# Filter chunks that write into their own inputs, in 512-column steps and with other gaps between them, and a Hyena result that is split in two halves

## The chip, the cores and the metric

The kernel runs on one core of one Trainium2 chip. The metric is the device time of one execution in microseconds (us), the median of the runs.

## What is computed

Two layers of a bidirectional encoder trunk on 256 positions of width 1024, all in float32. Each layer is a mixer and a SwiGLU feed-forward part, with an RMSNorm ahead of and behind each. Cut to what the change touches:

```python
def implicit_filters(L, w1, b1, fr1, w2, b2, fr2, w3):
    z, t = filter_features(L)
    h = jnp.sin(fr1.astype(jnp.float32) * (z @ w1.astype(jnp.float32) + b1.astype(jnp.float32)))
    h = jnp.sin(fr2.astype(jnp.float32) * (h @ w2.astype(jnp.float32) + b2.astype(jnp.float32)))
    h = (h @ w3.astype(jnp.float32)).reshape(L, 2 * HYENA_ORDER, HYENA_WIDTH).transpose(1, 2, 0)
...
    return h * decay[None]

def bidir_fft_conv(z, h_fwd, h_bwd, bias):
...
    kf = jnp.fft.rfft(k, axis=-1).T
    zf32 = z.astype(jnp.float32)
    zf = jnp.fft.rfft(zf32, n=2 * L, axis=1)
    y = jnp.fft.irfft(zf * kf[None], n=2 * L, axis=1)[:, :L]
    return (y + zf32 * bias.astype(jnp.float32)).astype(z.dtype)

def hybrid_mixer(u, pos, w_in, conv_w, conv_b, fw1, fb1, ff1, fw2, fb2, ff2, fw3, hy_bias,
                 w_o_attn, w_o_hyena, w_gate, b_gate, w_out):
...
    proj = u @ w_in
...
        o, l = dilated_window_attention(q[:, :, g], k[:, :, g], v[:, :, g], dil, window // (2 * dil))
...
    filt = implicit_filters(S, fw1, fb1, ff1, fw2, fb2, ff2, fw3)
    z = hx1 * bidir_fft_conv(hv, filt[0], filt[1], hy_bias[0])
    z = hx2 * bidir_fft_conv(z, filt[2], filt[3], hy_bias[1])
    y_hy = z @ w_o_hyena
...
    merged = gates[:, :, 0] * y_att.astype(jnp.float32) + gates[:, :, 1] * y_hy.astype(jnp.float32)
    return merged.astype(u.dtype) @ w_out
```

## The kernel before

**The main stream.** TensorE (PE) multiplies the activations by the weights in 128-row pieces, in the order in which the program is written. Every float32 product is three matmuls: high part by high part, high by low, low by high. A piece of weights comes by a DMA that SyncE (SP) issues (`raw`, L140, a ring of four buffers), ScalarE (ACT) makes its high part (`whi`, `hi_of`, L86), and VectorE (DVE) the low part (`wlo`, `lo_of`, L89); while `shared` holds, every fifth low part is made by GpSimd (POOL). The pieces of a projection into columns are 128x1024 (`wa`), those of q, k and v 128x768 (`wq`), worked off as 12 matmuls of 384 columns.

**The side jobs.** The filters, the FFT convolutions and the attention are generators. `tick()` (L98), which the main stream calls once for each piece, moves at most two of them on to their next `yield`. So the number of yields is the number of pieces that TensorE works off between two steps of a job. TensorE stays in program order; the instructions of DVE, ACT, POOL and SP are put in order by a scheduler when the kernel is built, and each engine then works off its list strictly in that order.

**A filter chunk** (`filter_chunk`, L280; for each layer four column groups `cc` and two filters `v`). SP loads `w3` (tile `w`, L282) and, into a single buffer, the bias row `bb` (L289). POOL makes the sum and the difference of the two halves of `w3` (`sd`, L294, L298), ACT and another engine split them (`sh`, `sl`, L303: DVE in layer 0, POOL in layer 1). The step "gst" (L309, L310) multiplies by the hidden features, DVE multiplies by the decay (`dd`, L313) and splits (`dh`, `dl`). The step "Z" (L326) is the transform by `fd`; `ev` (L330, L332) takes `bb` up, and four additions write the spectrum `K` (L335 to L339). Chunks with `l == 1 and cc == 2` (`late`) have four pieces ahead of gst, all others two; two pieces stand between gst and Z. The chunks of layer 0 run beside layer 0's first projections, those of layer 1 with `cc` 0 and 1 beside the feed-forward part of layer 0 and the rest beside the start of layer 1's mixer.

**A convolution** (`conv`, L539): POOL folds (`eo`, L543, L544), TensorE transposes (L549) and transforms (L559), DVE multiplies by `K` (L563 to L565), POOL adds (L566, L567, both 128x256), TensorE transforms back (L576, tile `inv`), POOL multiplies by the next factor (`X`, L584).

**An attention slot** (`attend`, L610): scores, softmax on DVE and ACT (`S`, L635 to L640), three pieces later the transposes of `S` (L648), then the product with v. The rotary embedding (`rt`, `qk`, L603 to L608) is POOL's. Ahead of slot 3 the whole Hyena result `X2` is split by `z_split` (L741): `zh` on ACT, `zl` on DVE, two halves of 128x1024.

Of the kernel before, what the change touches and what calls it, by code (L numbers as in the profile page):

```python
# [21 lines left out]
F32R = mybir.dt.float32r  # L22
BF16 = mybir.dt.bfloat16
AF = mybir.ActivationFunctionType
OP = mybir.AluOpType
# [19 lines left out]
def trunk(tc, nc, a, out):  # L45
# [4 lines left out]
    with es:  # L50
# [229 lines left out]
        def filter_chunk(l, v, cc, K, fd, shared):  # L280
# [22 lines left out]
            lo_of(sl, sd, sh, nc.gpsimd if l else None)  # L303
            for _ in range(4 if late else 2):
                yield
            Dh, Dl = [], []
            for e in range(2):
                h = acc()
                mm(h, gst[l][:, e, :], sh, True, False)  # L309
                mm(h, gst[l][:, e, :], sl, False, True)  # L310
                d = t512("dd")
                for q in range(2):
                    vtt(d[:, q * 256:(q + 1) * 256], h[:, q * 256:(q + 1) * 256], dec[:, e, :], op=OP.mult)  # L313
                dh, dl = r512("dh"), r512("dl")
                hi_of(dh, d)
                lo_of(dl, d, dh)
                Dh.append(dh)
                Dl.append(dl)
            yield
            yield  # L320
            hh, cq = cc // 2, cc % 2
            for s in range(2):
                z = acc()
                for e in range(2):
                    b = (2 * s + e) * P
                    mm3(z[:, e * 256:(e + 1) * 256], fd[:, b:b + P], fd[:, 512 + b:512 + b + P],  # L326
                        Dh[e][:, s * 256:(s + 1) * 256], Dl[e][:, s * 256:(s + 1) * 256], True, True)
                ev = f256("ev")
                if s == 0:
                    vtt(ev, z[:, 0:256], bb, op=OP.add)  # L330
                else:
                    nc.scalar.activation(ev, z[:, 0:256], AF.Copy)  # L332
                k0 = K[v][0][hh][:, cq * 512 + s * 256: cq * 512 + s * 256 + 256]
                k1 = K[v][1][hh][:, cq * 512 + s * 256: cq * 512 + s * 256 + 256]
                vtt(k0, z[:, 256:512], ev, op=OP.add)  # L335
                if s == 0:
                    vtt(k1, ev, z[:, 256:512], op=OP.subtract)
                else:
                    vtt(k1, z[:, 256:512], ev, op=OP.subtract)  # L339
            yield  # L340
# [198 lines left out]
        def conv(v, cc, z, xg, K):  # L539
# [16 lines left out]
            for j in range(2):  # L556
# [7 lines left out]
                vtt(t2[:, 0:256], zz[:, 0:256], Kt[:, 256:512], op=OP.mult)  # L564
                vtt(t2[:, 256:512], zz[:, 256:512], Kt[:, 0:256], op=OP.mult)  # L565
                ptt(t1[:, 0:256], t1[:, 0:256], t1[:, 256:512], op=OP.subtract)  # L566
                ptt(t1[:, 256:512], t2[:, 0:256], t2[:, 256:512], op=OP.add)  # L567
# [17 lines left out]
            yield  # L585
            yield
# [23 lines left out]
        def attend(s, qk, vt, OT):  # L610
# [30 lines left out]
            yield  # L641
            yield
            yield
# [30 lines left out]
        def mixer(l, U, o, K):  # L674
# [29 lines left out]
            convs = [4]  # L704
            X1 = [bigt(name="X1") for h in range(2)]
            X2 = [bigt(name="X2") for h in range(2)]
            for cc in range(4):
# [9 lines left out]
                def both(cc=cc, hvc=hvc, x1c=x1c, x2c=x2c):  # L717
                    yield from conv(0, cc, hvc, x1c, K)
                    yield from conv(1, cc, x1c, x2c, K)
                    convs[0] -= 1  # L720

# [17 lines left out]
            ZH, ZL = [], []  # L739

            def z_split():  # L741
                for h in range(2):
                    zh, zl = bigt(F32R, name="zh"), bigt(F32R, name="zl")
                    hi_of(zh, X2[h])
                    lo_of(zl, X2[h], zh)
                    ZH.append(zh)
                    ZL.append(zl)


            for s in (2, 3):  # L750
                att = slot(s, [bigt(name="qk") for i in range(2)], z_split if s == 3 else None)
# [242 lines left out]
```

## Time and profile before

| | |
|---|---|
| time, median of 3 runs (lowest to highest) | 1100.67 us (1100.32 to 1102.95) |
| the profiled execution | 1101.53 us |
| its span, first to last instruction | 1099.8 us |
| TensorE busy | 1077.7 us, 98% of the span |
| VectorE, ScalarE, GpSimd busy | 712.9, 554.0 and 394.1 us |
| mean granted TensorE clock | 0.998 of full speed |

The profiled execution lies 0.86 us above the median. TensorE is busy nearly all the time, so a change shows in the time only through the gaps in TensorE's work. A row of a timeline gives the start and the length of an instruction, or of a run of like ones (`x4`), and in brackets how long its engine was idle before it and what ended that.

### The profile page before, as it was taken

The page shows a single profiled execution, that of the slowest core. Times are in us where ns is not written, and L with a number is a line of the kernel's source. Part 1 is how long each engine was busy: PE and PEld are TensorE (multiplying, and loading weights), DVE is VectorE, ACT ScalarE, POOL GpSimd, SP SyncE. Part 2 cuts the span into 40 slices and gives each one's busy share as a digit, 9 for nine tenths or more (in the row PEclk, how much of TensorE's full clock was granted, in tenths as well). Part 3 has the DMA queues.
Part 4 walks back from the last instruction along what each step waited for, and adds up shares of the span by engine and source line. Part 5 has one row for each costly group of instructions (what it writes and reads, how often), then busy time and mean ns, then how long its engine had stood idle before and what let it go on. Part 6 is the DMA issues. An engine that isn't in the chain of part 4 may idle for free.

```text
span 1099.8 us, 18234 instructions
## 1 busy us (share of the span) xinstructions
PE 1077.7 (98%) x6984; PEld 1005.5 (91%) x6984; DVE 712.9 (65%) x1131; ACT 554.0 (50%) x828; POOL 394.1 (36%) x480
## 2 busy tenths in 40 slices
PE   8989999999999999999999999999999999999997
PEld 7989998899888899999889999998999889999986
DVE  5799986656646756665475877876445676554554
ACT  6555564443644645454465564444355455544442
POOL 2543123578713134211116714466645220111110
PEclk9999999999999999999999999999999999999999
DMA  8566544444446555656655544444455466555662
GB/s 295 177 207 196 163 140 141 151 132 128 145 163 199 185 183 185 194 179 222 198 171 172 179 148 141 133 158 150 129 158 187 164 219 191 156 189 177 206 192 77
DMA packets 60881, 189.21 MB, mean 172 GB/s; under 512 B 6903, under 2 KB 9337, under 8 KB 60794
## 3 DMA queue, kind: packets, MB, share of 16 engines
q1 hardware_dynamic: 60794, 188.04, 53.3%
q8 instruction: 55, 0.90, 0.3%
q14 instruction: 32, 0.26, 0.1%
HBM read 186.97 MB, written 1.05 MB: 171 GB/s over the span
## 4 chain that ended last, share of the span: by engine, by line
PE 88%; DVE 6%; DMA 2%; ACT 2%; issue 1%; POOL 1%; SPq 0%; DVEq 0%; POOLq 0%; ACTq 0%
PE acc L78 84%; DVE wlo L89 2%; PE acc L618 1%; DVE dl L89 1%; DMA mask<-in_mask_dram 1%; DVE dd L313 1%; ACT jk L350 1%; DMA raw<-in_wq_dram 1%; ACT whi L86 1%; PE acc L549 1%; PE acc L395 1%; PE acc L648 1%; DVE arg L239 1%; DMA w<-in_w_dram 0%; DVE X L371 0%
## 5 line engine op out<-in xcount | busy, mean ns | idle before, releaser
L86 ACT ACTIVATE whi<-raw 128x1024 fp32r<-128x1024 f32 (+1 forms) x352 | 346.3, 991 | 384.7 <-PE acc L78 292.0
L89 DVE TENSOR_TENSOR wlo<-raw,whi 128x1024 fp32r<-128x1024 f32 (+1 forms) x294 | 345.3, 1182 | 227.0 <-ACT whi L86 224.1
L78 PE MATMUL acc<-UH,whi 128*128 128x256 f32 x992 | 282.4, 285 | 0.0
L78 PE MATMUL acc<-UH,wlo 128*128 128x256 f32 x992 | 280.6, 283 | 0.0
L78 PE MATMUL acc<-UL,whi 128*128 128x256 f32 x992 | 280.6, 283 | 0.0
L89 POOL TENSOR_TENSOR wlo<-raw,whi 128x1024 fp32r<-128x1024 f32 (+1 forms) x58 | 132.9, 2292 | 405.2 <-ACT whi L86 405.1
L78 PE MATMUL acc<-whi,UH 128*128 128x384 f32 (+1 forms) x576 | 204.6, 355 | 0.0
L78 PE MATMUL acc<-wlo,UH 128*128 128x384 f32 (+1 forms) x576 | 202.0, 351 | 2.2 <-DVE wlo L89 1.4
L78 PE MATMUL acc<-whi,UL 128*128 128x384 f32 (+1 forms) x576 | 200.6, 348 | 0.0
L78 PEld LDWEIGHTS acc<-UL,whi 128*128 128x128 f32 x992 | 190.2, 192 | 0.4
L78 PEld LDWEIGHTS acc<-UH,whi 128*128 128x128 f32 x992 | 190.1, 192 | 0.4
L78 PEld LDWEIGHTS acc<-UH,wlo 128*128 128x128 f32 x992 | 190.1, 192 | 0.0
L78 PEld LDWEIGHTS acc<-wlo,UH 128*128 128x128 f32 x576 | 109.0, 189 | 9.8 <-DVE wlo L89 4.1
L78 PEld LDWEIGHTS acc<-whi,UH 128*128 128x128 f32 x576 | 109.1, 189 | 5.6 <-issue 0.7
L78 PEld LDWEIGHTS acc<-whi,UL 128*128 128x128 f32 x576 | 108.8, 189 | 5.4 <-DVE UL L89 0.2
L78 PE MATMUL acc<-whi,hs 128*128 128x512 f32 x352 | 109.0, 389 | 0.0
L78 PEld LDWEIGHTS acc<-whi,hs 128*128 128x128 f32 x352 | 66.1, 188 | 13.7
L78 PE MATMUL acc<-wlo,hs 128*128 128x512 f32 x176 | 68.5, 389 | 0.0
L828 DVE TENSOR_TENSOR HF<-acc,silu 128x256 f32<-128x256 f32 x38 | 16.1, 424 | 48.4 <-PE acc L78 48.4
L357 POOL TENSOR_SCALAR nv<-ss 128x1 f32<-128x1 f32 x16 | 7.1, 442 | 105.2 <-ACT jk L350 105.2
L78 PEld LDWEIGHTS acc<-wlo,hs 128*128 128x128 f32 x176 | 33.1, 188 | 6.7
L567 POOL TENSOR_TENSOR t<-t 128x256 f32<-128x256 f32 x32 | 36.5, 1142 | 4.3 <-DVE t L565 2.3
(168 smaller groups left out, 1570.1 us busy)
## 6 DMA issues: line engine op xcount, KB each, us to landing
raw<-in_wa_dram SPq DMA_DIRECT2D x240, 512.0 KB, 4.0
raw<-in_wq_dram SPq DMA_DIRECT2D x96, 384.0 KB, 3.5
raw<-in_wg_dram SPq DMA_DIRECT2D x16, 384.0 KB, 3.7
w<-in_w_dram SPq DMA_DIRECT2D x16, 256.0 KB, 4.2
gain<-in_gains_dram SPq DMA_DIRECT2D x7, 512.0 KB, 6.8
dec<-in_dec_dram SPq DMA_DIRECT2D x8, 256.0 KB, 3.1
bb<-in_hyb_dram SPq DMA_DIRECT2D x16, 128.0 KB, 3.3
gb<-in_bg_dram SPq DMA_DIRECT2D x8, 256.0 KB, 3.7
```

The lines of the kernel that those rows point to most:

```text
L78: nc.tensor.matmul(o, lT, r, start=start, stop=stop)
L86: return nc.scalar.activation(o, i, AF.Copy)
L89: (eng or nc.vector).tensor_tensor(o, i, h, op=OP.subtract)
L239: stt(arg, k, -c, arg, op0=OP.mult, op1=OP.add)
L313: vtt(d[:, q * 256:(q + 1) * 256], h[:, q * 256:(q + 1) * 256], dec[:, e, :], op=OP.mult)
L350: nc.scalar.activation(jk, half, AF.Square, scale=D ** -0.5, accum_out=ss[:, h:h + 1])
L395: nc.tensor.transpose(t[:, q * P:(q + 1) * P], u[:, h * 512 + q * P: h * 512 + (q + 1) * P], ident)
L549: nc.tensor.transpose(t[:, q * P:(q + 1) * P], eo[:, q // 2, q % 2, :], ident)
L567: ptt(t1[:, 256:512], t2[:, 0:256], t2[:, 256:512], op=OP.add)
L618: nc.tensor.transpose(t[:, q * P:(q + 1) * P], qk[i][:, j * 384 + g * P: j * 384 + (g + 1) * P], ident)
L648: nc.tensor.transpose(t[:, q * P:(q + 1) * P], S[:, i * 512 + q * P:i * 512 + (q + 1) * P], ident)
L828: vtt(ct(HF, f), ob, sl, op=OP.mult)
```

## The change

In `filter_chunk` the decayed product `dd` has no tile of its own: the first goes into `sd`, the second into `w`, and each is one 512-column instruction in place of two of 256. `ev` is one 512-column tile, and `K` is written by two 512-column instructions in place of four of 256. `sl` is made by POOL in both layers. The pieces ahead of gst and between gst and Z become 4 and 4 for `late` chunks, 3 and 3 in layer 0, and stay 2 and 2 for the other chunks of layer 1; the yield at the end goes in layer 0. In `conv` two 256-column products become one of 512 columns, and the two yields at the end stay for `v == 0` alone. Attention slot 2 gets a fourth piece between the softmax and the transposes. `z_split` takes one half: the first when two of the four convolution jobs are done, the second ahead of slot 3.

```diff
@@ filter_chunk
-            lo_of(sl, sd, sh, nc.gpsimd if l else None)
-            for _ in range(4 if late else 2):
+            lo_of(sl, sd, sh, nc.gpsimd)
+            for _ in range(4 if late else 2 if l else 3):
                 yield
             Dh, Dl = [], []
             for e in range(2):
                 h = acc()
                 mm(h, gst[l][:, e, :], sh, True, False)
                 mm(h, gst[l][:, e, :], sl, False, True)
-                d = t512("dd")
-                for q in range(2):
-                    vtt(d[:, q * 256:(q + 1) * 256], h[:, q * 256:(q + 1) * 256], dec[:, e, :], op=OP.mult)
+                d = (sd, w)[e]
+                vtt(d[:, :].rearrange("p (q c) -> p q c", q=2), h[:, :].rearrange("p (q c) -> p q c", q=2),
+                    dec[:, e:e + 1, :].to_broadcast([P, 2, 256]), op=OP.mult)
                 dh, dl = r512("dh"), r512("dl")
...
-            yield
-            yield
...
+            for _ in range(4 if late else 2 if l else 3):
+                yield
+
+            Z = []
+            for e in range(2):
                 z = acc()
...
+                for s in range(2):
+                    b, c = (2 * s + e) * P, slice(s * 256, (s + 1) * 256)
+                    mm3(z[:, c], fd[:, b:b + P], fd[:, 512 + b:512 + b + P], Dh[e][:, c], Dl[e][:, c], True, True)
+                if e == 0:
+                    ev = t512("ev")
+                    nc.scalar.activation(ev[:, 256:512], z[:, 256:512], AF.Copy)
+                    vtt(ev[:, 0:256], z[:, 0:256], bb, op=OP.add)
+                Z.append(z)
+
+            c = slice((cc % 2) * 512, (cc % 2) * 512 + 512)
+            vtt(K[v][0][cc // 2][:, c], Z[1], ev, op=OP.add)
+            vtt(K[v][1][cc // 2][:, c], ev, Z[1], op=OP.subtract)
+            if l:
+                yield
@@ conv
-                vtt(t2[:, 0:256], zz[:, 0:256], Kt[:, 256:512], op=OP.mult)
-                vtt(t2[:, 256:512], zz[:, 256:512], Kt[:, 0:256], op=OP.mult)
...
+                zv, kv, tv = (x.rearrange("p (s c) -> p s c", s=2) for x in (zz[:, :], Kt, t2[:, :]))
+                vtt(tv, zv, kv[:, ::-1, :], op=OP.mult)
...
-            yield
-            yield
+            if v == 0:
+                yield
+                yield
@@ attend
-            yield
-            yield
-            yield
+            for _ in range(4 if s == 2 else 3):
+                yield
@@ mixer
+            def z_split(h):
+                zh, zl = bigt(F32R, name="zh"), bigt(F32R, name="zl")
+                hi_of(zh, X2[h])
+                lo_of(zl, X2[h], zh)
...
                     convs[0] -= 1
+                    if convs[0] == 2:
+                        z_split(0)
...
-                att = slot(s, [bigt(name="qk") for i in range(2)], z_split if s == 3 else None)
+                att = slot(s, [bigt(name="qk") for i in range(2)], (lambda: z_split(1)) if s == 3 else None)
```

The scheduler also moves instructions whose code is unchanged. The first place is SP's list at the start of layer 1's mixer, where the last filter chunks are loaded: `w3` is the weights of a chunk, `bb` its bias row, `raw` a piece of the main stream. Before:

```order
L282 DMA w3_6852<-in_w3_dram 128x512 [waits Pool_49]
L140 DMA raw_6894<-in_wq_dram 128x768 [waits DMAHW1_49,DVE_49]
L282 DMA w3_6865<-in_w3_dram 128x512 [waits Pool_49]
L727 DMA gb_8307<-in_bg_dram 128x512 [waits DVE_49]
L140 DMA raw_6952<-in_wq_dram 128x768 [waits DMAHW2_49,DVE_49]
L289 DMA bb_6588<-in_hyb_dram 128x256 [waits DMAHW3_49,DVE_49]
L140 DMA raw_6988<-in_wq_dram 128x768 [waits DMAHW4_49,Pool_49]
L289 DMA bb_6856<-in_hyb_dram 128x256 [waits DMAHW5_49,DMAHW3_49,DVE_49]
```

And of the change:

```order
L140 DMA raw_6902<-in_wa_dram 128x1024 [waits DMAHW6_49,DVE_49]
L289 DMA bb_6488<-in_hyb_dram 128x256 [waits DMAHW4_49,DVE_49]
L282 DMA w3_6774<-in_w3_dram 128x512
L289 DMA bb_6778<-in_hyb_dram 128x256 [waits DMAHW4_49,DVE_49]
L282 DMA w3_6787<-in_w3_dram 128x512 [waits DMAHW7_49]
L140 DMA raw_6958<-in_wa_dram 128x1024 [waits DMAHW0_49,DVE_49]
```

The two `w3` of layer 1's `cc == 3` stood ahead of both `bb`; now each stands behind one, and a `bb` waits on DVE until the `ev` before it has read the single buffer.

The second place is POOL's list a little later, where the same two chunks are made ready for gst; `rt` is the rotary embedding of an attention slot. Before:

```order
L294 TENSOR_TENSOR sd_6869<-w3_6865 128x256
L298 TENSOR_TENSOR sd_6869<-w3_6865 128x256
L89 TENSOR_TENSOR wlo_6837<-raw_6834,whi_6836 128x768
L89 TENSOR_TENSOR sl_6862<-sd_6858,sh_6861 128x512
L89 TENSOR_TENSOR sl_6873<-sd_6869,sh_6872 128x512
L603 TENSOR_TENSOR rt_6817<-qk_6655,rope_87 128x48
```

And of the change:

```order
L298 TENSOR_TENSOR sd_6791<-w3_6787 128x256
L89 TENSOR_TENSOR sl_6784<-sd_6780,sh_6783 128x512
L605 TENSOR_TENSOR rt_6817<-qk_6555,rope_87 128x48
L606 TENSOR_TENSOR rt_6817<-qk_6555,rope_87 128x48
L607 TENSOR_TENSOR rt_6817<-qk_6555,rope_87 128x48
L608 TENSOR_TENSOR rt_6817<-qk_6555,rope_87 128x48
L605 TENSOR_TENSOR rt_6825<-qk_6556,rope_87 128x48
L606 TENSOR_TENSOR rt_6825<-qk_6556,rope_87 128x48
L607 TENSOR_TENSOR rt_6825<-qk_6556,rope_87 128x48
L608 TENSOR_TENSOR rt_6825<-qk_6556,rope_87 128x48
L89 TENSOR_TENSOR wlo_6887<-raw_6884,whi_6886 128x768
L89 TENSOR_TENSOR sl_6795<-sd_6791,sh_6794 128x512
```

Both `sl` stood ahead of the rotary embedding; now the second one stands behind eight of its instructions and a `wlo`.

The third place is POOL's list in layer 0, at the first convolutions (`v == 0`) of `cc` 2 and 3; L566 and L567 before are L564 and L566 or L568 after. Before:

```order
L566 TENSOR_TENSOR t1_2918<-t1_2918 128x256
L567 TENSOR_TENSOR t1_2918<-t2_2919 128x256
L566 TENSOR_TENSOR t1_2932<-t1_2932 128x256
L567 TENSOR_TENSOR t1_2932<-t2_2933 128x256
L566 TENSOR_TENSOR t1_2964<-t1_2964 128x256
```

And of the change:

```order
L564 TENSOR_TENSOR t1_2907<-t1_2907 128x256
L605 TENSOR_TENSOR rt_2932<-qk_2652,rope_87 128x48
L606 TENSOR_TENSOR rt_2932<-qk_2652,rope_87 128x48
L607 TENSOR_TENSOR rt_2932<-qk_2652,rope_87 128x48
L608 TENSOR_TENSOR rt_2932<-qk_2652,rope_87 128x48
L568 TENSOR_TENSOR t1_2894<-t2_2895 128x256
L605 TENSOR_TENSOR rt_2940<-qk_2653,rope_87 128x48
L606 TENSOR_TENSOR rt_2940<-qk_2653,rope_87 128x48
L607 TENSOR_TENSOR rt_2940<-qk_2653,rope_87 128x48
L608 TENSOR_TENSOR rt_2940<-qk_2653,rope_87 128x48
L566 TENSOR_TENSOR t1_2907<-t2_2908 128x256
L564 TENSOR_TENSOR t1_2954<-t1_2954 128x256
```

The four additions that the back transform of `cc` 2 reads stood together; now eight instructions of the rotary embedding of slot 2 stand between them.

## Rows read from the trace of the kernel before

**Rows 1.** The page, busy time of an engine, its share of the span and its instructions.

```profile
PE 1077.7 (98%) x6984; PEld 1005.5 (91%) x6984; DVE 712.9 (65%) x1131; ACT 554.0 (50%) x828; POOL 394.1 (36%) x480
```

**Rows 2.** The waits of TensorE: what waited, for what, us in total, times, longest.

```profile
PE acc L78 <- DVE dl L89: 6.9, 6, 2.3
PE acc L648 <- DVE S L640: 2.4, 1, 2.4
```

**Rows 3.** The timeline of TensorE at the filter chunks of layer 0: a low part of the piece behind the second gst, the first Z with its two waits, and a wait in the Z of `cc` 2.

```profile
57.69 0.34 PE L78 MATMUL acc<-wlo,UH 128*128 128x384 f32 x1
...
59.60 0.28 PE L78 MATMUL acc<-dh,fd 128*128 128x256 f32 x1
60.63 0.39 PE L78 MATMUL acc<-dl,fd 128*128 128x256 f32 x1 [0.76 <-DVE dl L89]
60.85 0.40 PE L78 MATMUL acc<-dh,fd 128*128 128x256 f32 x2
63.52 0.58 PE L78 MATMUL acc<-dl,fd 128*128 128x256 f32 x1 [2.27 <-DVE dl L89]
...
112.70 0.39 PE L78 MATMUL acc<-dl,fd 128*128 128x256 f32 x1 [1.76 <-DVE dl L89]
```

**Rows 4.** Stretches of the span: length, busy time and instructions of each engine, granted TensorE clock, DMA share and GB/s.

```profile
60.00:70.00 10.00, 7.10 (x37) 6.90 (x38) 8.85 (x17) 5.02 (x10) 8.59 (x17) 0.83 0.80 289
...
296.00:306.00 10.00, 7.61 (x53) 7.24 (x52) 6.99 (x10) 6.46 (x10) 2.93 (x2) 1.00 0.51 156
```

**Rows 5.** The timeline of DVE at the first filter chunks.

```profile
53.17 0.77 DVE L89 TENSOR_TENSOR sl<-sd,sh 128x512 fp32r<-128x512 f32 x1
...
70.62 2.20 DVE L89 TENSOR_TENSOR sl<-sd,sh 128x512 fp32r<-128x512 f32 x1 [0.54 <-ACT sh L86]
```

**Rows 6.** The timeline of POOL in the same stretch.

```profile
54.49 2.57 POOL L89 TENSOR_TENSOR wlo<-raw,whi 128x768 fp32r<-128x768 f32 x1
...
69.88 2.40 POOL L89 TENSOR_TENSOR wlo<-raw,whi 128x1024 fp32r<-128x1024 f32 x1
```

**Rows 7.** Groups of POOL's instructions, shapes apart: count, busy us, mean ns, idle before.

```profile
L89 POOL TENSOR_TENSOR wlo<-raw,whi 128x768 fp32r<-128x768 f32 x15 | 29.1, 1937 | 16.2 <-ACT whi L86 16.1
...
L89 POOL TENSOR_TENSOR sl<-sd,sh 128x512 fp32r<-128x512 f32 x8 | 10.5, 1318 | 4.5 <-ACT sh L86 4.5
```

**Rows 8.** The timeline of DVE at the softmax of slot 2 in layer 0.

```profile
292.54 2.54 DVE L89 TENSOR_TENSOR zl<-X,zh 128x1024 fp32r<-128x1024 f32 x2
...
298.83 1.98 DVE L640 TENSOR_SCALAR S<-S,rd 128x512 f32<-128x512 f32 x1
```

**Rows 9.** The timeline of TensorE there: the transposes of S.

```profile
300.96 0.63 PE L648 MATMUL acc<-ident,S 128*128 128x128 f32 x4 [2.39 <-DVE S L640]
```

**Rows 10.** The timeline of TensorE at the last filter chunks of layer 1: the first matmul of Z of `cc` 2, the first piece behind it and the first matmul of each of the two gst of `cc` 3.

```profile
603.34 0.28 PE L78 MATMUL acc<-dh,fd 128*128 128x256 f32 x1
...
608.64 0.34 PE L78 MATMUL acc<-whi,UH 128*128 128x384 f32 x1
...
616.97 0.39 PE L78 MATMUL acc<-sh,gst 128*128 128x512 f32 x1
...
617.89 0.39 PE L78 MATMUL acc<-sh,gst 128*128 128x512 f32 x1
```

**Rows 11.** The timeline of SP's DMA issues there.

```profile
599.53 0.42 SPq L282 DMA_DIRECT2D w<-in_w_dram  x1
...
601.72 0.42 SPq L282 DMA_DIRECT2D w<-in_w_dram  x1
...
607.90 0.33 SPq L289 DMA_DIRECT2D bb<-in_hyb_dram  x1
...
611.81 0.33 SPq L289 DMA_DIRECT2D bb<-in_hyb_dram  x1
```

**Rows 12.** The timeline of DVE there: the two `ev`.

```profile
607.46 0.41 DVE L330 TENSOR_TENSOR ev<-acc,bb 128x256 f32<-128x256 f32 x1
...
611.35 0.42 DVE L330 TENSOR_TENSOR ev<-acc,bb 128x256 f32<-128x256 f32 x1 [2.16 <-DMA bb<-in_hyb_dram]
```

**Rows 13.** The timeline of POOL there.

```profile
609.90 2.54 POOL L89 TENSOR_TENSOR sl<-sd,sh 128x512 fp32r<-128x512 f32 x2
612.40 0.29 POOL L603 TENSOR_TENSOR rt<-qk,rope 128x48 f32<-128x48 f32 x1
...
615.57 0.29 POOL L606 TENSOR_TENSOR rt<-qk,rope 128x48 f32<-128x48 f32 x1
```

**Rows 14.** The page's DMA issues of `w3`: instructions, KB each, median us from issue to landing.

```profile
w<-in_w_dram SPq DMA_DIRECT2D x16, 256.0 KB, 4.2
```

**Rows 15.** The timeline of TensorE at the first convolutions of `cc` 2 and 3 in layer 0: the first transform and the two back transforms.

```profile
242.88 0.28 PE L78 MATMUL acc<-nh,dft_h 128*128 128x256 f32 x1
...
249.90 1.95 PE L78 MATMUL acc<-inv,t 128*128 128x128 f32 x16
253.77 1.95 PE L78 MATMUL acc<-inv,t 128*128 128x128 f32 x16
```

**Rows 16.** The timeline of POOL there.

```profile
246.79 0.75 POOL L566 TENSOR_TENSOR t<-t 128x256 f32<-128x256 f32 x1
247.62 0.74 POOL L567 TENSOR_TENSOR t<-t 128x256 f32<-128x256 f32 x1
...
253.03 0.74 POOL L567 TENSOR_TENSOR t<-t 128x256 f32<-128x256 f32 x1
```

More of the change, by code (lines that the diff above doesn't have):

```diff
@@ L318, in filter_chunk @@
                 Dl.append(dl)
-            yield
-            yield
-            hh, cq = cc // 2, cc % 2
-            for s in range(2):
+            for _ in range(4 if late else 2 if l else 3):
+                yield
+            Z = []
+            for e in range(2):
                 z = acc()
[L324 to L339, printed above, removed]
-            yield
+                for s in range(2):
[11 more added lines that the diff above has]
+                yield
         def gain(l, n):
@@ L563, in conv @@
                 vtt(t1, zz, Kt, op=OP.mult)
-                vtt(t2[:, 0:256], zz[:, 0:256], Kt[:, 256:512], op=OP.mult)
-                vtt(t2[:, 256:512], zz[:, 256:512], Kt[:, 0:256], op=OP.mult)
-                ptt(t1[:, 0:256], t1[:, 0:256], t1[:, 256:512], op=OP.subtract)
-                ptt(t1[:, 256:512], t2[:, 0:256], t2[:, 256:512], op=OP.add)
+                zv, kv, tv = (x.rearrange("p (s c) -> p s c", s=2) for x in (zz[:, :], Kt, t2[:, :]))
+                vtt(tv, zv, kv[:, ::-1, :], op=OP.mult)
+                ptt(t1[:, 0:256], t1[:, 0:256], t1[:, 256:512], op=OP.add if j else OP.subtract)
+                if j:
+                    ptt(t1[:, 256:512], t2[:, 256:512], t2[:, 0:256], op=OP.subtract)
+                else:
+                    ptt(t1[:, 256:512], t2[:, 0:256], t2[:, 256:512], op=OP.add)
                 Y.append(t1)
@@ L640, in attend @@
                 nc.vector.tensor_scalar(Si, Si, rd, None, op0=OP.mult)
-            yield
-            yield
-            yield
+            for _ in range(4 if s == 2 else 3):
+                yield
             PT = bigt(name="PT")
@@ L704, in mixer @@
             convs = [4]
+            ZH, ZL = [], []
+            def z_split(h):
+                zh, zl = bigt(F32R, name="zh"), bigt(F32R, name="zl")
+                hi_of(zh, X2[h])
+                lo_of(zl, X2[h], zh)
+                ZH.append(zh)
+                ZL.append(zl)
             X1 = [bigt(name="X1") for h in range(2)]
@@ L738, in mixer @@
                     nc.scalar.activation(gt, gt, AF.Sigmoid)
[L739 to L747, printed above, removed]
             for s in (2, 3):
-                att = slot(s, [bigt(name="qk") for i in range(2)], z_split if s == 3 else None)
+                att = slot(s, [bigt(name="qk") for i in range(2)], (lambda: z_split(1)) if s == 3 else None)
                 queue.append(att)
```

## The prediction

> **What bounds the kernel now.** First the page's busy times: TensorE works 1077.7 of 1099.8 us [rows 1]. The change leaves every matmul of TensorE in place and only moves some, so what can be won is its waits, and what can be lost is new ones. Next the table of waits: TensorE waited 6.9 us, six times, for the low parts `dl` of the decayed filters, and once 2.4 us for the softmax of a slot [rows 2]. The timeline gives the places. Four of the six lie in layer 0: the first Z, due at 59.60, waits 0.76 and then 2.27 us, and a later one 1.76 us [rows 3]; the other two belong to layer 1's `cc == 2`. A wait costs more than its idle time: the matmul at 60.63 comes 1.03 us after the one ahead of it, where the pitch is 0.12 (two in 0.40, each 0.28 long), so 0.91 us are lost for 0.76 idle, 0.15 more. Last the stretches: behind the 2.27 us wait the granted clock of 60 to 70 us is 0.83, between the two levels of 1.2 and 2.4 GHz, which costs 0.17 of 10 us, 1.7 us. The stretch with the 2.4 us wait kept 1.00 [rows 4]. So I don't charge a clock drop to every wait.
>
> **What the change removes.** In all 6.9 + 2.4 of idle time, 7 x 0.15 for the restarts and 1.7 of clock: 12.1 us.
>
> The filters: gst to Z gets one more piece in layer 0 and two more for `late`. A 128x768 piece takes (616.97 - 608.64) / 4 = 2.08 us [rows 10]. In the first pair the second `dl` was 0.91 + 2.42 = 3.3 us late; one piece covers 2.1, and the rest comes from two `sl` of 0.77 us [rows 5] that leave DVE. The later waits are all under one piece. K, `ev` and `dd` in larger steps cost nothing: DVE does the same columns in fewer instructions, and waits for TensorE right after.
>
> The softmax: DVE had both halves of `zl` (2.54 us) ahead of it, and the last step ran to 300.81 [rows 8], for transposes that ended a wait of 2.39 us at 300.96 [rows 9]. One half of `zl` (1.27) goes to an earlier place, where nobody waits for it, and a fourth piece gives 2.08: 3.3 against 2.4 plus the restart. It goes.
>
> **What it adds.** Four places, all of which come from the order of POOL's and SP's lists.
>
> *The first pair.* POOL's `sl` (1.32 us [rows 7]) comes ahead of a `wlo` that ended at 54.49 + 2.57 = 57.06 [rows 6]. TensorE used it at 57.69 [rows 3]; now the second gst (0.92 us, 616.97 to 617.89 [rows 10]) stands behind that piece, so it is due at 56.76. Bounds: 0, if POOL begins earlier, and 57.06 + 1.32 - 56.76 = 1.6. I take 0.9, a little over the middle.
>
> *Convolutions of layer 0.* From the first transform to the back transform there are 7.0 us, to the next 3.9 [rows 15]. POOL's third addition ended at 247.54, the fourth at 248.36, 1.5 us early; the last of the second column group ended at 253.77, in the very moment of its use [rows 16]. Now eight rotary instructions stand between: 0.25 us each undisturbed, 3.5 for eight as they ran at 612.40 [rows 13]. Behind 247.54 come 2.0 to 3.5 of these and two additions of 0.75, so 251.0 to 252.5 against 249.90: 1.1 to 2.6 for `v == 0`, and as much at most for `v == 1`. Bounds 0 (the additions begin earlier) and 5.2; I take 1.5 and 0.7, 2.2, as the second column group catches up in part.
>
> *Convolutions of layer 1.* At two back transforms a POOL `wlo` (1.94 [rows 7]) and two `eo` of about 0.75 (same shape as the additions) come ahead of an addition. Against the slack of 1.5 that is 0 to 2.1 each; I take 0.75 each, 1.5.
>
> *The last filter chunks (`cc == 3` of layer 1).* Here the most is lost. Before, SP issued both `w3` at 599.53 and 601.72, well ahead of the two `bb` at 607.90 and 611.81 [rows 11], and POOL had both `sl` done at 612.44 [rows 13], 4.5 us before gst at 616.97. Now each `w3` stands behind a `bb` in SP's list, and a `bb` waits for the `ev` before it; the raw pieces behind them wait too, but the ring holds pieces enough for the four that follow. Counted from the start of Z of `cc` 2 (T): six matmuls of 0.12 and `ev` of 0.41 make T + 1.2; the first `bb` goes out. The second `ev` comes 611.35 - 607.90 = 3.45 us after that issue [rows 11, 12], at T + 4.7; second `bb` T + 5.1, second `w3` T + 5.4, landed 4.2 later [rows 14], T + 9.6. POOL's list puts both `sd` of it ahead of either `sl`: 2 x 0.75, then the first `sl`, 1.3: T + 12.4. gst is due after 24 x 0.12 of Z and 8.3 of pieces, T + 11.2: 1.2 late. For the second `sl` POOL first does eight rotary instructions (2.0 to 3.5), a `wlo` (1.9) and the `sl` (1.3): T + 17.6 to 19.1, due at 12.4 + 0.9 = 13.3: 4.3 to 5.8 late. Together 5.5 to 7.0; I take 6.0. Were SP not held up, this would be 0.
>
> The attentions of layer 1 also fall on other ticks; no row shows these, the bounds are 0 and one wait like that of rows 2 (2.4), and I take 0, as nothing longer is put ahead of their softmax.
>
> **The sum.** 1101.5 (the profiled execution) - 12.1 + 0.9 + 2.2 + 1.5 + 6.0 = 1100.0. That execution lies 0.9 over the median, so 1099.2 us: 0.13% under 1100.67. A measurement here tells about 0.3%, 3.3 us, from no change.
>
> **A rule that speaks against it.** DVE's `sl` of 128x512 took 0.77 us at 53.17, but 2.20 at 70.62, while POOL's `wlo` ran from 69.88 to 72.28 [rows 5, 6]: the DVE instruction ends 0.5 us after POOL's. The Trainium skill, GPSIMD Engine Reference, section 8 Key points, says that GpSimd shares its SBUF interfaces with VectorE, with contention for DVE instructions that have two SBUF inputs. By that rule, an `sl` of 1.32 us on POOL holds a `dl` or `wlo` of DVE for as long, and taking 0.77 from DVE wins nothing; these rows agree. The same page, section 4.1 Engine selection, has such elementwise work about twice as slow on GpSimd; 1.32 against 0.77 is 1.7 times.
>
> **The rivals.**
> - *The waits are swapped* (the sum): 1097.4 to 1103.5. Chance 0.44.
> - *The gain stays.* POOL and SP reach their lists' places sooner than worked out: T is later against POOL's other work, `w3` lands in the 3.4 us that a `bb` takes, or the rotary embedding is done in the first wait. Then the chunks of `cc == 3` cost 0 to 3 and the convolutions half: 1101.5 - 12.1 + 0.9 + 1.9 + 1.5 - 0.9 = 1092.8, between 1089 and 1097. For it: POOL is idle for most of the span [rows 1], and each gap that was short gets a whole piece. Against: the list of POOL is strict, and each step of the chain above has a row. Chance 0.38.
> - *Slower: `w3` late in layer 0 too.* There also the `w3` of a pair now stands behind a `bb`, and three pairs follow the first. A `bb` of 3.5 us, 4.2 for `w3` to land, 1.5 of `sd` and 1.3 of `sl` make 10.5 from the first `ev` on; from about 12.5 up, with `w3` landing in 6 us, gst would wait up to 1.5 to 2.5 in each pair. 1099.2 + 3 x 2 = 1105. Against: three pieces lie between the last Z of a pair and the next gst, and another between the two gst. Chance 0.11.
> - *DVE is not relieved* (the contention of the rows above): `dl` stays late in layer 0, and 5.0 idle, 0.6 of restarts and 1.7 of clock stay: 1099.2 + 7.3 = 1106.5. Against: a whole piece of slack comes on top, whatever DVE does. Chance 0.07.
>
> Faster 0.40 (0.38 and the lower edge of the sum), the same 0.42, slower 0.18 (the last two). Eight in ten lie between 1090 and 1105; the forecast's own range is 1097 to 1103.5.
>
> **What would show it.** In the table of waits `dl` and `S` should be gone, and the clock of the stretch around 60 us back at 1.00. In their place TensorE should wait for POOL's `sl` for 5 to 7 us in one or two waits in the first third of layer 1's mixer, and for `t` of POOL (the additions) four to six times, 3 to 4 us in all. If `sl` costs nothing there, the time is about 1093 and the chain over `bb` was wrong. If `sl` also shows in layer 0 more than once, the time is over 1103. If `dl` still waits in layer 0, DVE was held by POOL.

## The result and the profile after

The changed kernel takes 1115.99 us (median; 1115.21 to 1117.66), the kernel before in the same comparison 1101.45 us. The ratio is 1.0126, with a 95% interval of 1.011 to 1.0143: slower by 1.3%, where 1099.2 was forecast, and outside the range of 1090 to 1105. The profiled execution took 1115.21 us, with a span of 1113.4. One of the ten executions of run 3 below took 1774.99 us at a granted clock of 0.56; it is left out of every number.

First the page's busy times of the changed kernel, to be held against [rows 1].

```profile
PE 1081.5 (97%) x6984; PEld 1006.8 (90%) x6984; DVE 710.2 (64%) x1027; ACT 551.4 (50%) x828; POOL 404.0 (36%) x488
```

TensorE works off the same 6984 matmuls. DVE has 104 instructions less and 3 us less work; POOL has 10 us more. The span is 13.6 us longer. TensorE is idle for 9.8 us of that (span less busy time), and busy for 3.8 us more on the same matmuls, since some of them ran at a lower clock, as the stretches below show. The table of TensorE's waits of the changed kernel (what waited, for what, us, times, longest):

```profile
PE acc L78 <- POOL sl L89: 12.0, 7, 5.2
PE acc L78 <- POOL t L566: 3.4, 7, 1.0
PE acc L78 <- POOL wlo L89: 2.9, 2, 1.6
...
PE acc L78 <- POOL t L568: 1.8, 4, 1.0
```

`dl` and `S`, the two rows of [rows 2], are gone: their 9.3 us of idle time are won. But TensorE now waits for POOL, 20.1 us in all, where it waited 1.1 us before. Where these waits lie shows in its timeline (start, length, in brackets the idle time before it and what ended that): the piece between the first two gst of layer 0, a later gst, and the start of Z of `cc` 2 with the gst of `cc` 3 in layer 1, which answers to [rows 10].

```profile
58.07 0.44 PE L78 MATMUL acc<-wlo,UH 128*128 128x384 f32 x1 [1.56 <-POOL wlo L89]
...
106.65 0.50 PE L78 MATMUL acc<-sl,gst 128*128 128x512 f32 x1 [1.60 <-POOL sl L89]
...
609.34 0.28 PE L78 MATMUL acc<-dh,fd 128*128 128x256 f32 x1
...
620.53 0.40 PE L78 MATMUL acc<-sh,gst 128*128 128x512 f32 x1
624.17 0.50 PE L78 MATMUL acc<-sl,gst 128*128 128x512 f32 x1 [3.25 <-POOL sl L89]
...
630.53 0.80 PE L78 MATMUL acc<-sl,gst 128*128 128x512 f32 x1 [5.16 <-POOL sl L89]
```

The two waits in layer 1 hold 8.4 of the 12.0 us. The chain of the prediction can be read step by step from Z's start, its T, at 609.34. SP's issues there (to be held against [rows 11]):

```profile
611.45 0.33 SPq L140 DMA_DIRECT2D raw<-in_wa_dram  x1
611.88 0.38 SPq L289 DMA_DIRECT2D bb<-in_hyb_dram  x1
612.31 0.42 SPq L282 DMA_DIRECT2D w<-in_w_dram  x1
617.51 0.33 SPq L289 DMA_DIRECT2D bb<-in_hyb_dram  x1
617.89 0.42 SPq L282 DMA_DIRECT2D w<-in_w_dram  x1
```

DVE there: the last `wlo` ahead of the first `ev`, the two `ev` ([rows 12]), and the first split of `dl` behind gst.

```profile
610.46 0.96 DVE L89 TENSOR_TENSOR wlo<-raw,whi 128x768 fp32r<-128x768 f32 x1 [0.33 <-ACT whi L86]
611.34 0.41 DVE L331 TENSOR_TENSOR ev<-acc,bb 128x256 f32<-128x256 f32 x1
...
617.06 0.42 DVE L331 TENSOR_TENSOR ev<-acc,bb 128x256 f32<-128x256 f32 x1 [3.92 <-DMA bb<-in_hyb_dram]
...
627.08 2.28 DVE L89 TENSOR_TENSOR dl<-sd,dh 128x512 fp32r<-128x512 f32 x1
```

And POOL, from the first filter chunks to the last (for [rows 6] and [rows 13]); the `wlo` at 248.31 is one with no split of DVE beside it:

```profile
52.74 1.37 POOL L89 TENSOR_TENSOR sl<-sd,sh 128x512 fp32r<-128x512 f32 x1
...
56.00 2.02 POOL L89 TENSOR_TENSOR wlo<-raw,whi 128x768 fp32r<-128x768 f32 x1
...
101.97 2.42 POOL L89 TENSOR_TENSOR wlo<-raw,whi 128x1024 fp32r<-128x1024 f32 x1
104.36 2.24 POOL L89 TENSOR_TENSOR sl<-sd,sh 128x512 fp32r<-128x512 f32 x1
...
248.31 1.84 POOL L89 TENSOR_TENSOR wlo<-raw,whi 128x768 fp32r<-128x768 f32 x1
...
621.49 0.72 POOL L294 TENSOR_TENSOR sd<-w 128x256 f32<-128x256 f32 x1 [2.30 <-DMA w<-in_w_dram]
...
622.85 1.27 POOL L89 TENSOR_TENSOR sl<-sd,sh 128x512 fp32r<-128x512 f32 x1
...
626.04 2.78 POOL L89 TENSOR_TENSOR wlo<-raw,whi 128x768 fp32r<-128x768 f32 x1
628.78 1.70 POOL L89 TENSOR_TENSOR sl<-sd,sh 128x512 fp32r<-128x512 f32 x1
```

The second `w3` was issued at 617.89, 5.6 us behind the first, right after the `bb` ahead of it, which had waited for the second `ev`; run 6 below, where that `bb` need not wait, issues both `w3` together. POOL took it up at 621.49, and both `sl` come after that. Last the stretches (length, busy time of PE, its weight loads, DVE, ACT, POOL, the granted clock, DMA share, GB/s), for [rows 4]:

```profile
60.00:70.00 10.00, 10.00 (x65) 9.83 (x64) 8.17 (x10) 6.21 (x10) 7.85 (x13) 1.00 0.69 236
...
620.00:630.00 10.00, 2.13 (x9) 1.22 (x8) 6.16 (x7) 4.15 (x7) 8.51 (x13) 0.81 0.49 179
630.00:640.00 10.00, 9.46 (x43) 9.19 (x44) 5.46 (x7) 3.65 (x5) 1.91 (x5) 0.68 0.28 88
```

The clock is at 1.00 from 60 to 70 us, as forecast, but falls with the new waits: the mean is 0.81 from 620 to 630 us, where TensorE mostly waits, and 0.68 from 630 to 640 us, where it is busy again, which costs 3.2 us.

**The balance of the span**, in idle time plus 0.15 us for each restart: won 12.1 (as worked out ahead). New: the first pair 1.7, four later `sl` of layer 0 3.8, the attention behind the filters (L620) 0.8, convolutions of layer 0 5.1 and of layer 1 1.7, one `sl` in layer 1 at 600 us 0.5, the last filter chunks 8.7 and 3.2 of clock. That is 25.5 - 12.1 = 13.4 against 13.6 measured. Small waits that both kernels have are left out; each differs by 0.5 us at most.

### The profile page after: what moved, and what is told of

Read it like the earlier page. It is cut to its first block, busy times and chain, and to the rows that moved or that the text cites. A ratio compares the mean times of both kernels' runs of the same rounds, so it can differ in the third digit from the quotient of the medians.

```text
span 1113.4 us, 18172 instructions
## 1 busy us (share of the span) xinstructions
PE 1081.5 (97%) x6984; PEld 1006.8 (90%) x6984; DVE 710.2 (64%) x1027; ACT 551.4 (50%) x828; POOL 404.0 (36%) x488
## 4 chain that ended last, share of the span: by engine, by line
PE 81%; POOL 6%; DVE 4%; DMA 3%; issue 2%; ACT 2%; SPq 0%; POOLq 0%; DVEq 0%; ACTq 0%
PE acc L78 78%; DVE wlo L89 1%; POOL wlo L89 1%; DMA bb<-in_hyb_dram 1%; DMA w<-in_w_dram 1%; ACT whi L86 1%; PE acc L620 1%; POOL sl L89 1%; DMA raw<-in_wq_dram 1%; ACT jk L348 1%; PE acc L649 1%; PE acc L393 1%; PE acc L547 1%; POOL t L566 1%; POOL t L564 1%
## 5 line engine op out<-in xcount | busy, mean ns | idle before, releaser
L89 DVE TENSOR_TENSOR wlo<-raw,whi 128x1024 fp32r<-128x1024 f32 (+1 forms) x294 | 355.9, 1218 | 223.1 <-ACT whi L86 218.4
L89 DVE TENSOR_TENSOR hs<-HF,hs 128x256 fp32r<-128x256 f32 x44 | 33.2, 775 | 10.0 <-ACT hs L86 10.0
L78 PE MATMUL acc<-inv,t 128*128 128x128 f32 x256 | 34.5, 280 | 5.2 <-POOL t L566 3.4
```

Of the source, the lines that this page charges most:

```text
L78: nc.tensor.matmul(o, lT, r, start=start, stop=stop)
L89: (eng or nc.vector).tensor_tensor(o, i, h, op=OP.subtract)
```

## The experiments

Each ratio below is to the kernel before in the same comparison. Its median there was 1102.01 us for runs 1 to 4, 1101.35 for runs 5 to 8 and 1100.82 for runs 9 to 12, so differences between two runs are given by their times and come out up to 2 us otherwise by their ratios.

Two theories stood against each other. A: the waits for `sl` come from `w3`, which the scheduler now issues behind `bb`. B: they come from POOL, which is slow and does other things first. What put `w3` behind `bb` was also open. SP's list tells that without a run: when the parts of the change are taken back one by one, both `w3` move ahead of the `bb` only with the old code from Z on, or when `ev` alone gets a buffer of its own. With the latter SP's list reads:

```
L282 DMA w3_6774<-in_w3_dram 128x512
L282 DMA w3_6787<-in_w3_dram 128x512
...
L289 DMA bb_6488<-in_hyb_dram 128x256
L289 DMA bb_6778<-in_hyb_dram 128x256
```

The change takes `ev` from the ring of seven 512-column tiles that `w3` also comes from. The reading that fits is that the scheduler hands that ring out in program order, so the next chunk's `w3` has its place behind the last chunk's `ev`; how the scheduler decides it was not looked into further.

**1. A buffer of its own for `ev`.**

```diff
-                    ev = t512("ev")
+                    ev = sm.tile([P, 512], F32, tag="ev", bufs=1, name="ev")
...
-            return sm.tile([P, L], dt, tag="f256", bufs=4, name=name)
+            return sm.tile([P, L], dt, tag="f256", bufs=2, name=name)
```

> The changed kernel with one edit: `ev` gets a buffer of its own instead of one from the ring of 512-column tiles that `w3` also comes from (the ring of 256-column tiles is cut from four to two to make room). Both `w3` of each pair then stand ahead of the `bb` in SP's list, as before the change. Theory A (the `w3` held behind `bb` is what makes `sl` late): TensorE's waits for `sl` go in layer 1 (3.25 + 5.16 us and the slow clock behind them, 11.6 us together) and in layer 0 behind the first pair (3.8 us): 1116.0 - 15 = about 1101. Theory B (`sl` is late because POOL is slow and does other things first): the waits for `sl` stay at 8 us or more and the time over 1109.

Measured: 1111.73 us, ratio to the kernel before 1.01 (1.0079 to 1.0121). From its table of waits:

```profile
PE acc L78 <- ACT h L241: 3.6, 1, 3.6
PE acc L78 <- POOL sl L89: 2.9, 3, 1.4
```

Layer 1's two long waits for `sl` are gone, but TensorE waited 3.6 us for the filter's `h`, and the clock fell (0.73 from 40 to 50 us). Run 5, which keeps four 256-column tiles, has neither, so the cut of that ring to two is the likely reason. The time alone would have spoken for theory B; the waits speak for A. Run 5 repeats it without that shortage.

**2. `sl` on DVE in both layers**, with `w3` still behind `bb`.

```diff
-            lo_of(sl, sd, sh, nc.gpsimd)
+            lo_of(sl, sd, sh)
```

> The changed kernel with one edit: `sl` is made by DVE in both layers. SP's list still has `w3` behind `bb`. Theory A: in layer 1 the second `w3` lands 0.04 us before 621.5, `sd` takes 1.5, its high part about 0.6 and `sl` on DVE 0.7, so the second gst waits for about 2.7 us instead of 8.7 in two waits, and the clock does not drop; in layer 0 1.7 us at the first pair go and about half of the other 3.8: about 1104 to 1105, with 2 to 4 us of waits for `sl` left. Theory B: no wait for `sl` is left and the time is about 1100.

Measured: 1107.81 us, ratio 1.0067 (1.0047 to 1.0086).

```profile
PE acc L78 <- ACT sh L86: 2.6, 2, 1.4
...
PE acc L78 <- DVE sl L89: 1.3, 3, 0.5
```

As theory A has it, what is left of the waits (3.9 us for `sh` and `sl`, at 78 us and 621 to 624 us) is the late `w3`: even the high part `sh` is late now, and POOL begins the `sd` that it is made from as soon as `w3` is there (at 75.87, where the wait is ended by its DMA, and at 621.42, 3.65 us after its issue). The 1.6 us wait for `wlo` at the first pair is down to 0.2, so that one was `sl` on POOL. With `sl` on DVE in both layers the kernel is 8.2 us faster than the changed one (6.5 by the ratios); the late `w3` costs less, but it is not cured. Most of that lies in layer 1, whose `sl` was POOL's before the change too.

**3. The split in halves and slot 2's fourth piece alone**, in the kernel before (`z_split(0)` when two convolution jobs are done, four yields for slot 2).

> The kernel before with one part of the change: z_split in two halves and the fourth piece of slot 2. If the softmax wait was due to the two halves of `zl` ahead of it and is covered by a piece, TensorE's wait of 2.4 us for `S` goes and nothing else changes: ratio 0.9976, about 1098.5. If the first half disturbs the convolutions beside it: no change.

Measured: 1098.77 us, ratio 0.9975 (0.9961 to 0.9989). `S` is no longer in the table, and the waits for `dl` stay; the second view is the stretch behind the first pair's two waits:

```profile
PE acc L78 <- DVE dl L89: 7.9, 6, 2.3
```

```profile
60.00:70.00 10.00, 7.74 (x50) 7.53 (x51) 8.30 (x17) 4.92 (x9) 9.27 (x17) 1.00 0.75 254
```

The ratio is 2.7 us, which fits the 2.5 worked out. Not everything else stood still, though: the waits for `dl` are 1.0 us longer than in [rows 2], and the first pair's two waits, 0.75 and 2.26 us here, left the clock at 1.00, where 0.76 and 2.27 us went with 0.83 in [rows 4]. In this trace these two about cancel.

**4. The gaps alone**, in the kernel before.

```diff
-            for _ in range(4 if late else 2):
+            for _ in range(4 if late else 2 if l else 3):
                 yield
...
-            yield
-            yield
+            for _ in range(4 if late else 2 if l else 3):
+                yield
             hh, cq = cc // 2, cc % 2
```

> The kernel before with one part of the change: the numbers of pieces ahead of gst and between gst and Z (4 and 4 for late chunks, 3 and 3 in layer 0), nothing else. If one more piece is enough without taking `sl` from DVE, the waits for `dl` (6.9 us, 0.9 of restarts, 1.7 of slow clock) go: about 1092. If DVE is the limit, the first pair keeps 1 to 2 us of them: about 1094. New waits of the convolutions would show here too if they come from the changed phase of the jobs alone: then 1095 to 1098.

Measured: 1104.19 us, ratio 1.0024 (1.0007 to 1.0041): over the last of the cases.

```profile
PE acc L78 <- DVE nl L89: 3.2, 1, 3.2
PE acc L78 <- DVE wlo L89: 3.2, 6, 1.3
...
PE acc L78 <- DVE dl L89: 1.4, 2, 1.0
```

In layer 0 no `dl` is late any more although DVE makes every `sl` there: DVE was not the limit. But the jobs behind now fall on other ticks: a convolution's `nl` came 3.2 us late, with a stretch of slow clock (0.83 from 280 to 290 us), and in layer 1 `wlo` and `dl` are late again. The gaps alone win nothing.

**5. The code from Z on as before**, in the changed kernel: `ev` in two 256-column tiles of their old ring. In this run and in run 8 the odd half of the second spectrum has the old sign, which the changed additions take for the new one; the work is the same.

> The changed kernel with one edit: the code from Z on as before (`ev` in two 256-column tiles of their old ring of four, K in four additions), which takes `ev` out of the ring of `w3` without the shortage of 256-column tiles that cost the run e1_ev_own 3.4 us of a wait for `h` and as much of slow clock. Theory A: the waits for `sl` in layer 1 are gone as in e1_ev_own, the first pair of layer 0 keeps its wait for POOL's `wlo` (about 1.2 to 1.7), the convolutions keep theirs: 1116 - 11.6 - 2 = about 1102 to 1103. If POOL's rotary embedding or its speed were enough to make `sl` late: over 1109.

Measured: 1105.53 us, ratio 1.0039 (1.0026 to 1.0052). SP's issues in its trace, and the one wait for `sl` in its table:

```profile
589.98 0.90 SPq L282 DMA_DIRECT2D w<-in_w_dram  x2
...
610.24 0.33 SPq L289 DMA_DIRECT2D bb<-in_hyb_dram  x1
```

```profile
PE acc L78 <- POOL sl L89: 1.4, 1, 1.4
```

Both `w3` are issued 20 us ahead of the `bb`, and of seven waits for `sl` one is left, though POOL makes every `sl`. This is theory A, for layer 0 too: 10.5 us of the 14.5 that the change lost. The time is 2.5 us over what theory A gave; the one wait for `sl`, 0.4 us in the changed kernel, is 1.4 here, and the attention behind the filters (L624) waits 1.7 us where it waited 0.6.

**6. Two buffers for `bb`**, in effect: `bb` comes from the ring of 256-column tiles, enlarged to five.

```diff
-            bb = sm.tile([P, 256], F32, tag="bb", bufs=1, name="bb")
+            bb = f256("bb")
```

> The changed kernel with one edit: `bb` comes from the ring of 256-column tiles, enlarged to five, so no `bb` waits for the `ev` before it. `ev` stays in the ring of `w3`, and in SP's list both `w3` of `cc` 3 now stand behind a weight piece instead of a `bb`; POOL's list still has the second `sl` behind eight rotary instructions and a `wlo`. If the wait of `bb` is the greater part: the second `w3` is issued at about 612.4 instead of 617.9, the first wait for `sl` (3.25) falls to under 0.5, but the second stays at 4 to 5 since the rotary embedding waits for the piece just ahead of gst: about 1116 - 4 to 5 = 1111 to 1112. If the order of POOL alone makes the waits: no change in layer 1.

Measured: 1112.61 us, ratio 1.01 (1.0084 to 1.0115). POOL's second `sl` of `cc` 3, and TensorE's two waits:

```profile
626.59 1.70 POOL L89 TENSOR_TENSOR sl<-sd,sh 128x512 fp32r<-128x512 f32 x1
```

```profile
621.98 0.50 PE L78 MATMUL acc<-sl,gst 128*128 128x512 f32 x1 [1.20 <-POOL sl L89]
...
628.35 0.80 PE L78 MATMUL acc<-sl,gst 128*128 128x512 f32 x1 [5.18 <-POOL sl L89]
```

This tells the two halves of the chain apart. With `w3` not held by `bb`, the first `sl` ends at 621.9 instead of 624.1 and the first wait falls from 3.25 to 1.2, not under 0.5 as expected, since the first `w3`, issued at 611.83, reached POOL only at 617.17; the second wait stays at 5.2, since POOL's list has the rotary embedding and a `wlo` of 2.7 us ahead of the second `sl`. So the order of POOL is no cause beside SP's but its consequence: with `w3` early (run 5), POOL makes both `sl` ahead of these rotary instructions, at 612.75 to 615.29. In layer 0 the run changes little: a `bb` still goes out the moment an `ev` has ended (96.13 behind 96.10), and three of the four waits for `sl` stay, 2.9 of 3.2 us.

**7. Both yields at the end of `conv`**, as before the change.

```diff
-            if v == 0:
-                yield
-                yield
+            yield
+            yield
```

> The changed kernel with one edit: the two yields at the end of `conv` stay for both filters, as before the change. In POOL's list the four additions of the first back transform of `cc` 2 and 3 stand together again, behind the rotary embedding. If the rotary instructions between the additions make the convolutions' waits: the waits for `t` in layer 0 (about 3.4 + 1.9 us with restarts) go, and those of layer 1 (2) perhaps: 1116 - 5 to 7 = 1109 to 1111. If they come from the filters being late: no change.

Measured: 1110.64 us, ratio 1.0078 (1.0062 to 1.0094).

```profile
PE acc L78 <- POOL t L566: 1.1, 2, 0.9
...
PE acc L78 <- POOL t L568: 0.2, 1, 0.2
```

The waits for `t` fall from 5.2 us in eleven waits to 1.3 in three, all in layer 1. So it is the two pieces that the change takes from the end of a convolution that put the next pair's additions among the rotary embedding of slot 2. A new wait of 1.0 us for DVE (`G`, L624) comes in an attention.

**8. The three undone together**: old code from Z on, `sl` of layer 0 on DVE, both yields in `conv`. The gaps, `dd` in 512-column steps and in place, the merged `t2` and the halves stay.

> The changed kernel with the three suspects undone together: the code from Z on as before (so `w3` is early), `sl` of layer 0 on DVE as before, both yields at the end of `conv`. What stays of the change: the gaps between the steps, `dd` in 512-column steps in place, the merged `t2`, the fourth piece of slot 2 and the split in halves. If these three make all the new waits: 1101.5 - 12.1 = 1089 to 1092. If the gaps bring waits of their own by moving the later jobs, as in e4_gaps_only (3.3 us at a convolution, 3.2 in layer 1): 1095 to 1098.

Measured: 1098.72 us, ratio 0.9977 (0.9967 to 0.9986).

```profile
PE acc L78 <- POOL sl L89: 1.2, 1, 1.2
PE acc L78 <- ACT h L241: 1.2, 1, 1.2
PE acc L78 <- POOL t L570: 1.1, 2, 0.9
```

The 17 us against the changed kernel are these three causes: 10.5 in run 5, 5.4 in run 7 and 1.7 at the first pair make 17.6. But of the 12 us that were to be won against the kernel before, only 2.6 are. The rest is mostly in small waits at new places, eleven of 0.2 to 1.2 us each (for `h`, `sl`, the additions, the attention of layer 0), like those of run 4.

**9. As 8, with `sl` on DVE in layer 1 too**, and the sign of K put right.

> e8_three_undone with two edits: `sl` is made by DVE in layer 1 too, and the second half of K has the sign that the changed additions of the convolution need (in e5_old_z and e8_three_undone it had the sign of the kernel before, so a part of the spectrum was negated; the instructions and their shapes are the same). If POOL's `sl` makes the one wait for `sl` that e8_three_undone kept (1.24 us at 594 us, in layer 1), it goes and nothing else changes: about 1097. If DVE then holds up something else: 1098.5 to 1100.

Measured: 1098.52 us, ratio 0.9972 (0.9956 to 0.9987): no different from run 8. The wait for `sl` at 596 us stays at 0.8 us with DVE as the one waited for. It beats both kernels, as run 3 does with much less.

**10 and 11. Run 3 with four pieces between gst and Z of the late chunks**; and in addition one more piece in the first column group of layer 0.

```diff
-            yield
-            yield
+            for _ in range(4 if late else 2 if l or cc else 3):
+                yield
             hh, cq = cc // 2, cc % 2
```

> e3_split_only with one more part of the change: four pieces between gst and Z for the late chunks of layer 1 (layer 0 stays at two). The two waits for `dl` there (0.5 and 1.4 us with 0.3 of restarts) should go: 1099.0 - 2.2 = about 1096.8. If the later Z moves the jobs behind it so that POOL's lists or DVE come late (as in e4_gaps_only, 1.3 + 1.0 + 0.4 us at 620 to 628 us): about 1099.

Measured: 1101.10 us, ratio 1.0006 (0.9996 to 1.0015), 2.3 us slower than run 3 (3.4 by the ratios). DVE's timeline in layer 1, the waits, and the stretch behind the first pair's waits:

```profile
615.36 3.66 DVE L89 TENSOR_TENSOR wlo<-raw,whi 128x768 fp32r<-128x768 f32 x2
```

```profile
PE acc L78 <- DVE dl L89: 4.4, 4, 2.3
PE acc L78 <- DVE wlo L89: 3.2, 6, 1.5
```

```profile
60.00:70.00 10.00, 7.47 (x34) 7.26 (x35) 8.47 (x17) 4.57 (x9) 8.52 (x16) 0.66 0.80 265
```

The two waits for `dl` of `cc` 2 in layer 1 go (1.9 us), but two `wlo` behind that Z took 3.66 us together, beside a POOL `wlo`, and a wait for `wlo` of 1.5 us, two for `dl` of `cc` 3 (1.4) and three for `t` in layer 1's convolutions (1.3) take their place. Two waits for `dl` of 1.5 us each in layer 0 go as well, but behind the first pair's waits, the same as before, the clock is 0.66 here and was 1.00 in run 3. So the later Z wins nothing; what it costs by itself, the traces don't tell.

> e10_split_late with one more piece between gst and Z in the first column group of layer 0 alone. The first pair's waits for `dl` (0.75 + 2.27 us, 0.3 of restarts, and the slow clock where it fell) should go: 3 to 5 us under e10_split_late. If the phase of the later jobs decides, they bring new waits of 1 to 4 us at the convolutions or attentions of layer 0, and the gain is under 2 us.

Measured: 1103.36 us, ratio 1.002 (1.0007 to 1.0033). That is 2.3 us slower than run 10, where 3 to 5 us faster, or a gain of less than 2, was expected. The first pair's two waits (0.76 and 2.27 us) are down to one of 1.2, with the clock at 1.00 behind it, but `dl` is late six times more, 4.5 us, at later chunks, with the clock at 0.83 from 130 to 140 us. That fits the second case, in which the phase of the jobs decides, and goes further.

**12. Tiles of their own for the decayed products.**

```diff
-                d = (sd, w)[e]
+                d = t512("dd")
```

> The changed kernel with one edit: the decayed products get tiles of their own from the ring of 512-column tiles, instead of overwriting `sd` and `w`. SP's list keeps `w3` behind `bb`. Theory A (only `ev` in that ring puts `w3` behind `bb`, the overwriting has no part in it): no change against the changed kernel, about 1116, with the waits for `sl` in layer 1 at 8 us or more. If the overwriting holds the tiles that `w3` needs: 5 us or more faster.

Measured: 1116.32 us, ratio 1.0138 (1.0119 to 1.0157), the changed kernel's time. That the chunks overwrite their inputs neither wins nor loses anything that shows.

## Why the prediction was wrong

**What held.** The 12.1 us to be won: `dl`, `S` and the slow stretch at 60 us went. (The 1.7 us for that stretch were one execution's: with the same two waits run 3's trace has a clock of 1.00 there and run 10's 0.66.) The places of the losses: the first pair, both kinds of convolution, the last filter chunks. The chain of the last chunks runs as written, step by step. The forecast was that the waits are swapped; they were, at 25.5 us instead of the 10.6 in the sum. Of the 14.9 us between them 5.9 lie at the last chunks, 3.8 in layer 0's late `w3`, 2.9 in layer 0's convolutions and 2.3 elsewhere. The term of layer 1's convolutions, 1.5 taken and 1.7 measured, was partly luck: it came by five waits of 0.2 us with their restarts, not by two of 0.75.

**The term of the last chunks** was put at 6.0 and measured 8.7 us of waits and 3.2 of slow clock. Four steps were too small. The first `ev` ended at T + 2.4 instead of T + 1.2, since two `wlo` stood ahead of it on DVE (the second until 611.42). From the first `bb`'s issue to the second `ev` it took 617.06 - 611.88 = 5.2 us instead of the 3.45 of [rows 11, 12]; in SP's new order the `bb` goes out 0.4 us behind a weight piece of 512 KB, which is the likely reason, but no run varies that alone. POOL's `wlo` and second `sl` took 2.78 and 1.70 instead of 1.9 and 1.3, while DVE split `dl` beside them, in 2.28 us. And no clock drop was charged, because the 2.4 us wait of [rows 4] had brought none; here the clock fell in the second of two waits that have only four matmuls between them, and runs 6, 7 and 12, which have the same two, show the same (0.69 to 0.72 in the 10 us from about the second wait's end).

The contention is the one that the prediction saw in [rows 5, 6], but it goes both ways: POOL's `wlo` is stretched from 1.84 us (at 248.31) to 2.78 as well as DVE's `dl`. The Trainium skill, GPSIMD Engine Reference, section 8 Key points, says that GpSimd shares its SBUF interfaces with VectorE; this trace agrees.

**The step that failed altogether** is the third rival, `w3` late in layer 0 too, which got a chance of 0.11. It came: four waits for `sl` behind the first pair, 3.8 us. The rival's terms, with a `bb` of 3.5 us behind the first `ev`, are those of the second `w3` of a pair. Three of the four waits (0.9, 1.6 and 0.3 us) are for the first `w3`, for which no chain was written. SP's issues and DVE's `ev` ahead of the wait at 106.65:

```profile
96.44 0.33 SPq L289 DMA_DIRECT2D bb<-in_hyb_dram  x1
96.82 0.43 SPq L282 DMA_DIRECT2D w<-in_w_dram  x1
```

```profile
96.00 0.41 DVE L331 TENSOR_TENSOR ev<-acc,bb 128x256 f32<-128x256 f32 x1
```

The Z of this `ev` had begun at 90.26, but DVE had `wlo` pieces and the main stream's short convolutions ahead of it, so it ended only at 96.41. The first `w3` went out 0.4 us later, and gst needed its `sl` at 105.05, 8.6 us behind the `ev`. POOL took `w3` up at 100.58 and made `sd` (1.4 us), a `wlo` (2.4) and then `sl` (2.2), which ended at 106.60. The objection counted the pieces between Z and gst, but neither how late `ev` comes behind Z nor what POOL has in front of `sl`. For layer 1 the same effect was taken into the sum. One cause, `w3` behind `bb`, was priced at one of its places and made a rival at the other.

**The convolutions of layer 0** were worked out as 1.1 to 2.6 for each filter, and then 2.2 was taken for both, as the second column group was to catch up. Measured are 5.1 us, next to the upper bound of 5.2. Run 7 shows the mechanism to be the one described. The first pair's 1.7 (0.9 taken, bound 1.6) is POOL's `sl` ahead of `wlo`, as run 2 shows. In three of four places the value lay at the upper bound or over it. One engine's list, POOL's, has a part in all of them, so the terms were hardly independent, as the range treated them; that this is why they all came out high is a reading that no run tests.

**The contention as a rival.** That DVE would be held by POOL so that `dl` stays late did not come: `dl` is gone from the table, and run 4 shows that a whole piece is enough even with `sl` on DVE. So no run shows a gain from the move of layer 0's `sl` to POOL; it cost 1.7 us at the first pair (run 2), and behind a late `w3` some more, which no run separates from the rest.

## What to carry to other kernels

When a scheduler orders the queues, a tile that moves to another ring changes the order of the loads that share the ring: read the list of the issuing engine for every load behind a load that waits, and price that at every place where the pattern stands. Where several new waits come from one engine's list, take them to come out high or low together. When TensorE is 98% busy and the side jobs are placed by counting pieces, more room at one step moves all the later ones; a part that removes one wait and moves little else (here the split in halves, 2.7 us) is worth more than one that shifts phases.

## What the runs showed of the hardware

POOL's split of 128x768 took 1.84 us with no split of DVE beside it and 2.78 us where DVE split a piece and then `dl`; that `dl`, 0.7 us elsewhere in the trace, took 2.28. A `bb` of 128 KB was used 3.45 us after its issue in [rows 11, 12] and 5.2 us after it in the changed kernel, where a 512 KB load had gone out 0.4 us ahead of it.

Whether a wait of TensorE drops the clock is not told by its length: one of 2.4 us did not [rows 4], and in run 4 one of 3.2 us did. Nor do the same waits always give the same clock. Behind one of 0.76 us and one of 2.27 the stretch of 60 to 70 us had 0.83 in the kernel before [rows 3, 4], 0.66 in run 10, and 1.00 in run 3 with 0.75 and 2.26. A term for the clock that is read from one trace is therefore uncertain by its whole size.
